# A hybrid decoder step on one core: token halves instead of quarters, another start of pair 1, and a written order for evictions, taps and weight parts

## Chip, cores and metric

One core of a Trainium2 chip runs the whole program. The metric is device time in microseconds (us), the median of several runs; a profile is one further execution. Engines: PE (matmul), PEld (its weight loads), DVE, ACT, POOL, and SP, whose queue issues all DMA transfers here.

## What is computed

One decoder layer for 1024 prompt tokens and 32 sample tokens (8 sequences of 4), 1056 columns in all, model width 1024. The part that the change touches is the end of the mixer and the feed-forward block:

```
x = x + (sig(gA)*A@w_br_ret + sig(gB)*B@w_br_sg + sig(gC)*C@w_br_x) @ w_o
z  = rmsnorm(x) @ w_up                    # 1024 -> 2*2816
zc = conv_b + sum(conv_w[j] * zp[:, j:j+L] for j in range(3))   # causal, zp = [history, z]
a, b = split(zc, 2)
x = x + (gelu(a) * b) @ w_down;  y = rmsnorm(x)
```

Outputs are y, the retention states, the last two rows of z for each sequence (the convolution's state), and the key/value caches.

## The kernel before

Activations lie transposed: 128 partitions of channels, tokens along the columns. Each fp32 product is made of three matmuls in the type fp32r: a value is cast to a high part (ACT), the rest is the low part (a subtraction, on POOL or DVE), and high*high, high*low, low*high are added up in PSUM. The helpers record most operations, so profile lines are theirs: mm is L106, act L109, vtt (DVE tensor-tensor) L112, ptt (POOL tensor-tensor) L115, stt (DVE scalar-tensor-tensor) L118, dma L103.

**Columns.** In the attention projection w_o (loop at L1337, two passes of eight output tiles) and in the up projection the 1056 columns are two halves of 528, each two quarters of 264 (256 prompt tokens and 8 sample tokens). So the residual tile x2c is read from DRAM and written to it (scx) by two DMAs a tile, one for the 256s and one for the 8s; the gated sum mg is split by two casts and two subtractions (split_q, L305); and an eviction of a product to z takes two operations, one for the prompt and one for the samples (z_put, L1400).

**Up projection.** Its 44 output tiles are taken as 22 pairs: tile j of a (gelu side) and tile 22+j of b. Pair 0 is a plain product. Pairs 1 to 21 use Winograd's form of Strassen's scheme: input rows in two halves, tokens in two halves, so seven products (prod, L1379) instead of eight. A product is 4 row blocks x 3 terms x 2 chunks = 24 matmuls. The weight blocks are a11, a12 (first slab), a21, a22 (second slab) and the sums s1 = a21+a22, s2 = s1-a11, s3 = a11-a21, s4 = a12-s2; the column operands are the plain blocks B11, B21, B12, B22 and T1 to T4 (differences of them, made once by t1, t2, t2l, t3 from L1480 and split by T1s, T3s, T4s). The products are, in this order, a11*B11, s2*T2, a12*B21, s3*T3, s1*T1, s4*B22, a22*T4. f_prep (L1298) loads nothing itself: it makes s1, s2 on DVE and s3, s4 on POOL, casts three pieces of 1024 columns and a22 on ACT, subtracts on POOL, and lets f_dma fetch the next pair's two slabs into the two buffers wr.

**PSUM and evictions.** A product has one of three PSUM buffers in turn (L1382), so a product waits for the eviction of the third one before it. a11 is evicted by ACT into p1 (first half of tile zt); s2 by DVE as r = s2 + p1 (second half of zt); s3 as u3 and s1 as u4 (tile zu), s1 once more into z of b, s4 into z of a, a22 into z of b, a12 into z of a.

**Convolution.** For each of the two tiles, ACT makes c = w2*z + bias (for 1024 prompt columns and 32 sample columns, L109) and copies the state columns; DVE adds two taps, each one operation of 1024 columns and one of 32 (L118); ACT applies gelu to the a side; DVE multiplies (c<-c, 1056 columns) and a DMA stores the result to sca.

**What sets the order.** In before, code order on each engine follows a small scheduler. convs and preps are queues of generators; after (L1591), called behind each product, advances convs by one or two steps, then preps by one, then up to four entries of todo. conv_a runs to the end (with gelu) before conv_b begins. For pair 0, todo (L1501) is a list of steps, one taken per row block of six matmuls; the steps that are left are run before pair 1, and T3s, T1s, T4s are put behind. In the last pair first_down (L1570) starts the down projection's loads.

Of the kernel before, what the change touches and what calls it, by code (L numbers as in the profile page):

```python
# [71 lines left out]
QW = 264  # L72
HW = 2 * QW

# [4 lines left out]
def step_kernel(ctx: ExitStack, tc: tile.TileContext, xT, memT, wslab, cst, ident_d, rope, vec, sgc, sgm, sgs,  # L79
# [215 lines left out]

    def q_parts(t):

        v = quarters(t)
        return v[:, :, 0:256], v[:, :, 256:QW]

    def t_parts(t):

        return t[:, 0:TP].rearrange("p (q c) -> p q c", c=256), t[:, TP:T].rearrange("p (q c) -> p q c", c=8)

    def split_q(src, name):  # L305

        hi = slot(name + "h", F32R)
        lo = slot(name + "l", F32R)
        for h, l, s in zip(q_parts(hi), q_parts(lo), t_parts(src)):
            nc.scalar.copy(out=h, in_=s)  # L310
            ptt(l, s, f(h), ALU.subtract)
        return hi, lo
# [57 lines left out]
    with tc.manual_schedule():  # L370
# [927 lines left out]
        def f_prep(j):  # L1298
            if j >= NFF:
                return  # L1300
            wa, wb = fraw.pop(j)
            a11, a12, a21, a22 = wa[:, 0:512], wa[:, 512:1024], wb[:, 0:512], wb[:, 512:1024]
            sa, sb = slot("fs"), slot("fs")
            s2, s3, s1, s4 = sa[:, 0:512], sa[:, 512:1024], sb[:, 0:512], sb[:, 512:1024]
            d = fw[j] = {}

            def parts(names, src):
                hi = wp.tile([P, 1024], F32R, tag="wh", name="wh", bufs=3)
                lo = wp.tile([P, 1024], F32R, tag="wl", name="wl", bufs=3)
                nc.scalar.copy(out=hi, in_=src)  # L1310
                ptt(lo, src, f(hi), ALU.subtract)
                for i, n in enumerate(names):
                    d[n] = (hi[:, 512 * i:512 * i + 512], lo[:, 512 * i:512 * i + 512])

            def sum12():
                vtt(s1, a21, a22, ALU.add)
                vtt(s2, s1, a11, ALU.subtract)

            def sum34():
                ptt(s3, a11, a21, ALU.subtract)  # L1320
                ptt(s4, a12, s2, ALU.subtract)

            def last22():
                t = slot("f22", F32R)
                nc.scalar.copy(out=t[:, 0:512], in_=a22)
                ptt(t[:, 512:1024], a22, f(t)[:, 0:512], ALU.subtract)
                d["a22"] = (t[:, 0:512], t[:, 512:1024])
                f_dma(j + 1)

            p0 = lambda: parts(("a11", "a12"), wa)  # L1330
            p1 = lambda: parts(("s2", "s3"), sa[:, 0:1024])
            p2 = lambda: parts(("s1", "s4"), sb[:, 0:1024])
            for fn in (p0, sum12, sum34, last22, p1, p2) if j == 1 else (sum12, sum34, p0, last22, p1, p2):
                fn()
                yield

        for half in range(2):  # L1337
            rate[0] = 0.25
            for m in range(8):
# [27 lines left out]
                for i, o in zip(q_parts(x2c[m]), t_parts(scx[m])):  # L1367
                    dma(o[:, 2 * half:2 * half + 2], i[:, 2 * half:2 * half + 2])
# [10 lines left out]
        def prod(w, name, ps=None, start=True, stop=True, tick=None):  # L1379

            if ps is None:
                ps = bpp.tile([P, 2, 512], F32, tag="bp", name="bp", bufs=3)  # L1382
            wh, wl = [x.rearrange("p (k c) -> p k c", c=P) for x in w]
            for k in range(4):
                xh, xl = xop(name, k)
                for i, (a, r) in enumerate(((wh, xh), (wh, xl), (wl, xh))):
                    for q in range(2):
                        mm(ps[:, q, 0:QW], a[:, k, :], r[:, q * QW:(q + 1) * QW], start=(start and k == 0 and i == 0),
# [10 lines left out]

        def z_put(ps, half, z, zs, tmp=None):  # L1400

            oz = z[:, 2 + 512 * half:514 + 512 * half].rearrange("p (q c) -> p q c", c=256)
            os_ = zs[:, 4 * half:4 * half + 4, 2:6].rearrange("p (q i) t -> p q i t", q=2)
            iz = ps[:, :, 0:256]
            is_ = ps[:, :, 256:QW].rearrange("p q (i t) -> p q i t", i=2)
            if tmp is None:
                nc.scalar.copy(out=oz, in_=iz)
                nc.scalar.copy(out=os_, in_=is_)
            else:
                tv = quarters(tmp)  # L1410
# [119 lines left out]
        while todo:  # L1530
            do()
# [391 lines left out]
```

## Time and profile before

| what | value |
|---|---|
| median of 3 runs | 1989.2 us (1988.41 to 1991.27) |
| profiled execution | 1988.9 us |
| its span, first to last instruction | 1987.1 us |
| mean granted TensorE clock | 0.988 |
| busy: PE / DVE / ACT / POOL | 95% / 53% / 31% / 47% of the span |
| HBM read, written | 137.04 MB, 35.43 MB |

The profile names operations by line and by tile: bp is the PSUM buffer of the up projection, mp that of the others; xh, xl are high and low parts of the column operands, wh, wl those of weights, f the split a22, wr raw weight slabs, fs the weight sums, z and zs up-projection results of prompt and samples, c the convolution's results, opr a result read back from sca, x (x2) the residual. In a timeline a row gives start, duration, engine, line, operation, out<-in, shapes, how many were merged, and in brackets how long the engine had been idle and what ended that.

### The profile page before, as it was taken

What the parts mean: (1) busy time and instruction counts of PE and PEld (TensorE: products, weight loads), DVE (VectorE), ACT (ScalarE), POOL (GpSimd) and SP (SyncE); (2) the same over time, 40 slices, a digit from 0 to 9 for tenths busy, and PEclk for the clock granted to TensorE, in tenths of its full rate; (3) what the DMA queues carried; (4) which work ended last, traced back from release to release, by engine and by line L of the source; (5) the groups of instructions that cost most, each with busy time, mean ns of one, the idle gap of its engine ahead of it and who ended that gap; (6) DMA issues with size and microseconds to landing.
All of it is one profiled execution on the core that took longest, in us unless ns stands there. A gap on an engine that the chain in (4) does not pass through costs nothing. (4 is left out here: it accounts for less than half of the span.)

```text
span 1987.1 us, 31577 instructions
## 1 busy us (share of the span) xinstructions
PE 1888.2 (95%) x13201; PEld 1854.9 (93%) x13201; DVE 1057.2 (53%) x1507; ACT 615.4 (31%) x962; POOL 927.9 (47%) x596
## 2 busy tenths in 40 slices
PE   7999999999899999999999998799999999899997
PEld 6999999999899999999999997699999999899996
DVE  8463636442555532111112268788888888744437
ACT  5223222422134432111222244344333434321104
POOL 7242433231633334333254465765666566664404
PEclk9999999999999999999999999899999999999999
DMA  5112131314132323111221641122222223642202
GB/s 180 54 43 88 43 110 43 120 55 149 59 133 99 97 87 97 43 43 43 99 84 43 205 128 54 65 65 65 65 80 82 65 70 100 230 140 99 95 1 88
DMA packets 65438, 174.52 MB, mean 88 GB/s; under 512 B 14288, under 2 KB 25712, under 8 KB 65296
## 3 DMA queue, kind: packets, MB, share of 16 engines
q1 hardware_dynamic: 65296, 172.50, 26.7%
q8 instruction: 104, 1.70, 0.4%
q14 instruction: 38, 0.31, 0.1%
HBM read 137.04 MB, written 35.43 MB: 87 GB/s over the span
## 5 line engine op out<-in xcount | busy, mean ns | idle before, releaser
L115 POOL TENSOR_TENSOR wl<-wr,wh 128x1024 fp32r<-128x1024 f32 x115 | 281.9, 2454 | 399.1 <-ACT wh L150 377.2
L106 PE MATMUL mp<-hh,wh 128*128 128x384 f32 (+1 forms) x1152 | 263.7, 337 | 9.9 <-ACT hh L109 5.0
L106 PE MATMUL mp<-hl,wh 128*128 128x384 f32 (+1 forms) x1152 | 254.0, 328 | 4.3 <-DVE hl L118 4.3
L106 PE MATMUL mp<-hh,wl 128*128 128x384 f32 (+1 forms) x1152 | 251.4, 326 | 0.0
L106 PE MATMUL bp<-xh,wh 128*128 128x264 f32 x1072 | 221.2, 288 | 24.2 <-DVE zt L112 16.1
L106 PE MATMUL bp<-xh,wl 128*128 128x264 f32 x1072 | 219.7, 286 | 6.7 <-POOL wl L115 6.7
L106 PE MATMUL bp<-xl,wh 128*128 128x264 f32 x1072 | 220.4, 287 | 5.1 <-DVE xl L112 3.5
L106 PEld LDWEIGHTS mp<-hh,wh 128*128 128x128 f32 x1152 | 192.4, 191 | 12.7 <-ACT rsh L351 5.1
L106 PEld LDWEIGHTS mp<-hl,wh 128*128 128x128 f32 x1152 | 193.5, 190 | 6.7 <-DVE hl L118 6.7
L106 PEld LDWEIGHTS bp<-xh,wh 128*128 128x128 f32 x1072 | 167.8, 190 | 28.9 <-DVE zt L112 19.9
L106 PEld LDWEIGHTS mp<-hh,wl 128*128 128x128 f32 x1152 | 193.5, 190 | 0.0
L118 DVE SCALAR_TENSOR_TENSOR c<-z,hist,c 128x1024 f32<-128x1024 f32 x88 | 154.9, 1760 | 50.0 <-ACT c L109 47.7
L106 PEld LDWEIGHTS bp<-xh,wl 128*128 128x128 f32 x1072 | 167.9, 190 | 7.4 <-POOL wl L115 7.4
L106 PEld LDWEIGHTS bp<-xl,wh 128*128 128x128 f32 x1072 | 167.5, 190 | 7.3 <-DVE xl L112 5.2
L112 DVE TENSOR_TENSOR x<-x,mp 128x288 f32<-128x288 f32 (+3 forms) x167 | 105.7, 675 | 122.2 <-PE mp L106 118.1
L115 POOL TENSOR_TENSOR wl<-fs,wh 128x1024 fp32r<-128x1024 f32 x42 | 113.3, 2698 | 50.3 <-ACT wh L1310 47.0
L150 ACT CAST wh<-wr 128x1024 fp32r<-128x1024 f32 x100 | 103.9, 1041 | 79.8 <-PE mp L106 50.0
L106 PE MATMUL mp<-ach,whs 128*128 128x384 f32 (+3 forms) x524 | 123.5, 325 | 4.8 <-DVE x L112 3.8
L106 PE MATMUL mp<-ach,wls 128*128 128x384 f32 (+3 forms) x524 | 123.5, 325 | 0.0
L106 PE MATMUL mp<-acl,whs 128*128 128x384 f32 (+3 forms) x524 | 123.0, 324 | 0.0
L112 DVE TENSOR_TENSOR th<-mp,rst 128x768 f32<-128x768 f32 (+1 forms) x48 | 31.7, 701 | 170.9 <-PE mp L106 150.3
L118 DVE SCALAR_TENSOR_TENSOR th<-th,mp 128x768 f32<-128x768 f32 (+1 forms) x48 | 31.7, 701 | 145.4 <-PE mp L106 145.4
(341 smaller groups left out, 4069.6 us busy)
## 6 DMA issues: line engine op xcount, KB each, us to landing
wr<-in_wslab SPq DMA_DIRECT2D x164, 512.0 KB, 3.6
sca<-c SPq DMA_DIRECT2D x22, 528.0 KB, 5.6
opr<-sca SPq DMA_DIRECT2D x22, 528.0 KB, 4.6
opr<-scr SPq DMA_DIRECT2D x16, 528.0 KB, 5.4
scr<-ort SPq DMA_DIRECT2D x8, 528.0 KB, 8.3
x<-scx SPq DMA_DIRECT2D x8, 528.0 KB, 10.6
s<-in_sret SPq DMA_DIRECT2D x8, 512.0 KB, 6.2
out_srets<-s SPq DMA_DIRECT2D x8, 512.0 KB, 3.5
```

The costliest lines, as they stand in the source:

```text
L106: nc.tensor.matmul(out=out, lhsT=l, rhs=r, start=start, stop=stop)
L112: nc.vector.tensor_tensor(out=out, in0=a, in1=b, op=op)
L115: nc.gpsimd.tensor_tensor(out=out, in0=a, in1=b, op=op)
L118: nc.vector.scalar_tensor_tensor(out=out, in0=a, scalar=s, in1=b, op0=op0, op1=op1)
L150: nc.scalar.copy(out=hi, in_=raw)
```

## The change

- Half 0 of the columns is now tokens 0 to 527, half 1 tokens 528 to 1023 and the 32 samples. x2c is loaded by one DMA a tile and stored by one a half; mg is split by one cast and one subtraction.
- Half 0 of z is one eviction of 528 columns. In half 1 the products on B12, B22 and T1 have chunks of 248 and 280 columns, so that prompt (2 x 248) and samples (32) are two operations; s1's eviction to u4 also becomes two.
- Pair 1 has its own code and product order: a11, a12, s4, s2, s3, s1, a22. todo goes on through its products. The sums of pair 1 are made on POOL, every second low part of half 1 as well, and all splits of T1, T3, T4; s1, s4 of pair 1 get buffers of their own (fh, fl). Since s4 comes first there, u4 is added to z of a by two extra additions later.
- Pairs 2 to 21 have a written order: tap steps of both tiles alternate with the evictions, the first step of conv b does not wait for gelu of conv a, and the four weight parts of the next pair stand behind a12, s1, s4 and at the head of the next pair. The next pair's slabs are fetched from there.
- In pair 21 the steps of first_down stand behind a12, s3, s1, s4 and a22 (before: behind a11, s2, a12, s3, s1).

DVE, a pair in the middle: the rows from the last eviction of one pair (z of a22) to the eviction of s2 (zt) in the next, before:

```order
L112 TENSOR_TENSOR z<-bp,zu 128x512
L112 TENSOR_TENSOR zs<-bp,zu 128x4x4
L118 SCALAR_TENSOR_TENSOR c<-z,hist,c 128x1024
L118 SCALAR_TENSOR_TENSOR c<-zs,hist,c 128x32
L118 SCALAR_TENSOR_TENSOR c<-z,hist,c 128x1024
L118 SCALAR_TENSOR_TENSOR c<-zs,hist,c 128x32
L118 SCALAR_TENSOR_TENSOR c<-z,hist,c 128x1024
L118 SCALAR_TENSOR_TENSOR c<-zs,hist,c 128x32
L112 TENSOR_TENSOR fs<-wr 128x512
L112 TENSOR_TENSOR fs<-fs,wr 128x512
L112 TENSOR_TENSOR zt<-bp,zt 128x528
```

And the same place now, up to the eviction of a12 (z<-bp,zt):

```order
L112 TENSOR_TENSOR z<-bp,zu 128x528
L118 SCALAR_TENSOR_TENSOR c<-z,hist,c 128x1024
L118 SCALAR_TENSOR_TENSOR c<-zs,hist,c 128x32
L118 SCALAR_TENSOR_TENSOR c<-z,hist,c 128x1024
L118 SCALAR_TENSOR_TENSOR c<-zs,hist,c 128x32
L112 TENSOR_TENSOR zt<-bp,zt 128x528
L118 SCALAR_TENSOR_TENSOR c<-z,hist,c 128x1024
L118 SCALAR_TENSOR_TENSOR c<-zs,hist,c 128x32
L112 TENSOR_TENSOR z<-bp,zt 128x528
```

zt moves ahead of conv b's first tap and of the weight sums, which now stand behind both of conv b's taps.

POOL at the start, from the first weight part of pair 1 (wl<-wr) on; xl are low parts of column operands, wl, fl and f of weights. Before:

```order
L115 TENSOR_TENSOR wl<-wr,wh 128x1024
L115 TENSOR_TENSOR fs<-wr 128x512
L115 TENSOR_TENSOR fs<-wr,fs 128x512
L115 TENSOR_TENSOR f_10993<-wr,f_10993 128x512
L115 TENSOR_TENSOR xl<-x2c,xh 128x528 x2
L115 TENSOR_TENSOR wl<-fs,wh 128x1024
L115 TENSOR_TENSOR xl<-x2c,xh 128x528 x4
L115 TENSOR_TENSOR wl<-fs,wh 128x1024
L115 TENSOR_TENSOR xl<-x2c,xh 128x528
L1417 MEMSET z 128x2
L1418 COPY zs<-hist 128x8x2
L115 TENSOR_TENSOR xl<-x2c,xh 128x528 x4
```

And now:

```order
L115 TENSOR_TENSOR wl<-wr,wh 128x1024
L115 TENSOR_TENSOR xl<-x2c,xh 128x528 x4
L115 TENSOR_TENSOR fl<-fs,fh 128x1024
L115 TENSOR_TENSOR wl<-fs,wh 128x1024
L115 TENSOR_TENSOR f_11148<-wr,f_11148 128x512
L115 TENSOR_TENSOR xl<-x2c,xh 128x528 x8
L1411 MEMSET z 128x2
L1412 COPY zs<-hist 128x8x2
L115 TENSOR_TENSOR xl<-x2c,xh 128x528 x4
L115 TENSOR_TENSOR wl<-wr,wh 128x1024
```

All weight parts of pair 1 stand ahead of the twelve xl of T3, T1 and T4, and the first part of pair 2 behind them; the sums moved ahead of this piece.

SP in pair 21: from the store of pair 19's result (sca) to the first loads of the residual (x), before:

```order
L103 DMA sca_10912<-c 128x1056
L103 DMA opr<-sca_10893 128x1056
L103 DMA opr<-sca_10894 128x1056
L103 DMA wr<-in_wslab 128x1024 x4
L103 DMA opr<-sca_10895 128x1056
L103 DMA opr<-sca_10896 128x1056
L103 DMA x_16286<-scx_192 128x1056
```

And now:

```order
L103 DMA sca_10872<-c 128x1056
L103 DMA opr<-sca_10853 128x1056
L103 DMA opr<-sca_10854 128x1056
L103 DMA wr<-in_wslab 128x1024 x4
L103 DMA sca_10873<-c 128x1056
L103 DMA opr<-sca_10855 128x1056
L103 DMA opr<-sca_10856 128x1056
L103 DMA x_16291<-scx_192 128x1056
```

The store of pair 20's result stands ahead of the residual now.

The diff, cut to its core:

```diff
-QW = 264
-HW = 2 * QW
+HW, QW = 528, 264
+HA, HB = 248, 280
...
-            mops.append(split_q(acc[m], "mg"))
+            mops.append(split(acc[m], "mg"))
...
-            for o, i in zip(q_parts(x2c[m]), t_parts(xT[m])):
-                dma(o, i)
+            dma(x2c[m], xT[m])
...
+            ch = ((0, 0, HA), (1, HA, HB)) if name in ("B12", "B22", "T1") else ((0, 0, QW), (1, QW, QW))
...
+        def put_t(ps, out, tmp):
+            vtt(n496(out), ps[:, :, 0:HA], n496(tmp), ALU.add)
+            vtt(out[:, 2 * HA:HW], ps[:, 1, HA:HB], tmp[:, 2 * HA:HW], ALU.add)
...
+            if half == 0:
+                put(ps, z[:, 2:2 + HW], tmp)
+                return
...
-        T1s = lambda k: x_split("T1", k, h(k, 0), vtt if k < 2 else ptt)
+        T1s = lambda k: x_split("T1", k, h(k, 0), ptt)
...
-            lambda: (norm_sums(1), one()), one, one, None, None, lambda: norm_root(1), one,
+            lambda: (norm_sums(1), f_sums(1, ptt)()), lambda: f_prep0(1), None, None, None, None, lambda: norm_root(1),
...
+        put(prod(d["a11"], "B11", tick=do), p1)
+        n = prod(d["a12"], "B21", tick=do)
...
+        n = prod(d["s4"], "B22", tick=do)
...
+        put(prod(d["s2"], "T2", tick=do), r, p1)
+        pa.first()
+        pa.tap(1)
+        put(prod(d["s3"], "T3", tick=do), u3, r)
...
-        for j in range(1, NFF):
+        for j in range(2, NFF):
...
+            f_prep3(j)
...
+            pb.first()
+            pa.tap(1)
...
+            put(prod(d["a11"], "B11"), p1)
+            ticks()
+            pa.tap(0)
+            pa.gelu()
+            put(prod(d["s2"], "T2"), r, p1)
+            ticks()
+            pb.tap(1)
             n = prod(d["a12"], "B21")
...
+                f_prep0(j + 1)
+            pb.tap(0)
+            s34 = None if last else f_sums(j + 1, vtt)
+            put(prod(d["s3"], "T3"), u3, r)
...
+                s34()
+            conv_end(j - 1, pa, pb)
             n = prod(d["s1"], "T1")
...
+                f_prep1(j + 1)
             n = prod(d["s4"], "B22")
             z_put(n, 1, *za, u4)
...
+            conv[0].first()
...
+                f_prep2(j + 1)
             n = prod(d["a22"], "T4")
             z_put(n, 0, *zb, u3)
```

Here first is the ACT step of a convolution, tap(1) and tap(0) its two DVE steps, conv_end the product and the store; f_prep0 to f_prep3 split (a11, a12), (s2, s3), (s1, s4) and a22, f_prep3 fetching the next slabs; f_sums makes s1, s2 and returns the function that makes s3, s4 on POOL.

More of the change, by code (lines that the diff above doesn't have):

```diff
@@ L1296, in f_dma, with f_parts @@
                     dma(t, wslab[SLABS.index(key)])
[L1298 to L1307, printed above, removed]
+        def f_parts(j, names, src, own=False):
+            if own:
+                hi, lo = slot("fh", F32R, [P, 1024]), slot("fl", F32R, [P, 1024])
+            else:
@@ L1319, in sum34 @@
[L1319 to L1335, printed above, removed]
+            nc.scalar.copy(out=hi, in_=src)
+            ptt(lo, src, f(hi), ALU.subtract)
+            for i, n in enumerate(names):
+                fw[j][n] = (hi[:, 512 * i:512 * i + 512], lo[:, 512 * i:512 * i + 512])
+        def f_quads(j):
+            return [t[:, 512 * i:512 * i + 512] for t in fraw[j] for i in range(2)]
@@ new lines, in step_kernel, with f_sums, f_prep0 @@
+        fsum = {}
+        def f_sums(j, sub):
+            a11, a12, a21, a22 = f_quads(j)
+            fsum[j] = (slot("fs"), slot("fs"))
+            s2, s3, s1, s4 = [t[:, 512 * i:512 * i + 512] for t in fsum[j] for i in range(2)]
+            sub(s1, a21, a22, ALU.add)
+            sub(s2, s1, a11, ALU.subtract)
+            return lambda: (ptt(s3, a11, a21, ALU.subtract), ptt(s4, a12, s2, ALU.subtract))
+        def f_prep0(j):
+            fw[j] = {}
+            f_parts(j, ("a11", "a12"), fraw[j][0])
@@ new lines, in f_prep1, with f_prep2, f_prep3 @@
+        def f_prep1(j, own=False):
+            f_parts(j, ("s2", "s3"), fsum[j][0][:, 0:1024], own)
+        def f_prep2(j, own=False):
+            f_parts(j, ("s1", "s4"), fsum[j][1][:, 0:1024], own)
+        def f_prep3(j):
+            a22 = f_quads(j)[3]
+            t = slot("f22", F32R)
+            nc.scalar.copy(out=t[:, 0:512], in_=a22)
+            ptt(t[:, 512:1024], a22, f(t)[:, 0:512], ALU.subtract)
+            fw[j]["a22"] = (t[:, 0:512], t[:, 512:1024])
+            del fraw[j]
+            f_dma(j + 1)
@@ L1366, in step_kernel @@
                     vtt(s, s, sq[:, 0:HW], ALU.add)
[L1367 to L1368 removed]
+                dma(scx[m][:, half * HW:(half + 1) * HW], hs(m, half))
             drain()
@@ L1464, in ticks @@
                 wait.pop(0)[1]()
-        def turn_to(q, n):
-            for _ in range(n):
-                turn(q)
         h = hs
@@ new lines, in step_kernel, with first_down @@
+        pb.tap(0)
+        conv_end(0, pa, pb)
+        def first_down():
+            a_load(0)
+            a_load(1)
+            w_dma()
+            w_dma()
+            yield
+            a_split(0)
+            w_prep()
+            yield
+            a_split(1)
+            w_prep()
+            yield
+            a_load(2)
+            a_load(3)
+            x2_load(range(4))
+            yield
+            x2_load(range(4, 8))
+            yield
+        for j in range(2, NFF):
+            last = j == NFF - 1
+            pa, pb = conv
+            if j == 2:
+                pa.first()
+            d = fw[j]
+            f_prep3(j)
+            fw.pop(j)
+            pb.first()
+            pa.tap(1)
+            p1, r, u3, u4 = blocks(j)
```

255 lines of the change are left out of this document (111 added, 144 removed).

## The prediction

> **What bounds the kernel now.** I read the page first, for the busy share of each engine, then the waits of PE, a table by stretches, and the timelines of one pair, of the start and of the end. An execution took 1988.9 us with the profiler on: this span and 1.8 us around it.
>
> ```profile
> span 1987.1 us, 31577 instructions
> ...
> PE 1888.2 (95%) x13201; PEld 1854.9 (93%) x13201; DVE 1057.2 (53%) x1507; ACT 615.4 (31%) x962; POOL 927.9 (47%) x596
> ```
>
> PE is busy 95% of the span, so only its idle time and its slow time can be won. The waits of PE in the whole run (us in total, times, longest) say what ends that idle time:
>
> ```profile
> PE bp L106 <- DVE zt L112: 16.1, 18, 0.9
> ...
> PE bp L106 <- POOL wl L115: 6.7, 3, 3.9
> ...
> PE bp L106 <- ACT wh L1310: 5.3, 1, 5.3
> ...
> PE bp L106 <- DVE zu L112: 4.1, 2, 3.8
> ...
> PE mp L106 <- POOL mgl L115: 1.2, 1, 1.2
> ```
>
> The first comes 18 times at 0.9 us: once a pair. The next three are a few long waits. The table by stretches places them: from the end of the attention projection to pair 3, pairs 3 to 20, pair 21, and the first down-projection group.
>
> ```profile
> 1197.90:1294.00 96.10, 74.75 (x531) 71.29 (x532) 80.35 (x87) 40.74 (x73) 61.27 (x37) 0.91 0.16 52
> 1294.00:1685.50 391.50, 375.42 (x3028) 370.20 (x3028) 324.74 (x396) 152.67 (x249) 245.53 (x180) 1.00 0.24 73
> 1685.50:1709.50 24.00, 21.16 (x171) 20.58 (x170) 20.16 (x23) 10.47 (x19) 14.67 (x9) 1.00 0.35 113
> 1709.50:1726.00 16.50, 12.68 (x76) 12.17 (x77) 12.49 (x13) 6.57 (x9) 10.19 (x4) 1.00 1.03 399
> ```
>
> The first stretch has PE idle for 21 of 96 us, at a granted clock of 0.91: the long waits stand there, and DVE is busy 80 us of it. In the second PE is idle only by the short wait. The PE timeline gives the marks: pair 3 begins at 1294.20, pair 21 at 1685.47, the down projection at 1709.41.
>
> ```profile
> 1294.20 0.40 PE L106 MATMUL bp<-xh,wh 128*128 128x264 f32 x2
> ...
> 1425.20 0.40 PE L106 MATMUL bp<-xh,wh 128*128 128x264 f32 x2
> ...
> 1435.89 0.40 PE L106 MATMUL bp<-xh,wl 128*128 128x264 f32 x2
> 1437.20 0.51 PE L106 MATMUL bp<-xh,wh 128*128 128x264 f32 x2 [0.90 <-DVE zt L112]
> ...
> 1685.47 0.41 PE L106 MATMUL bp<-xh,wh 128*128 128x264 f32 x2
> ...
> 1709.41 0.72 PE L106 MATMUL mp<-ach,whs 128*128 128x384 f32 x3 [0.96 <-DVE zs L112]
> ```
>
> A pair takes (1685.47 - 1294.20)/18 = 21.74 us. From 1425.20 to 1435.89 lie 44 rows of two matmuls, 0.1215 us each, so a product (24) takes 2.92 and seven 20.4. The row at 1437.20 starts 1.31 after the one before instead of 0.24, and its first two matmuls take 0.1 longer: the wait costs 1.17 a pair, and a pair without it takes 20.57. It is s1 waiting for a PSUM buffer: three are in turn, and s1 needs the one from which DVE evicts s2 into zt.
>
> **Why that eviction is late, and what DVE and POOL share.** Rows of the same pair on ACT, DVE and POOL, in order of time:
>
> ```profile
> 1423.37 1.24 ACT L109 ACTIVATE c<-z,hist 128x1024 f32<-128x1024 f32 x1 [7.44 <-DVE zs L112]
> ...
> 1425.36 1.28 DVE L118 SCALAR_TENSOR_TENSOR c<-z,hist,c 128x1024 f32<-128x1024 f32 x1
> ...
> 1426.14 2.76 POOL L115 TENSOR_TENSOR wl<-fs,wh 128x1024 fp32r<-128x1024 f32 x1 [1.70 <-ACT wh L1310]
> ...
> 1426.55 2.40 DVE L118 SCALAR_TENSOR_TENSOR c<-zs,hist,c 128x32 f32<-128x32 f32 x1
> ...
> 1428.86 1.29 POOL L115 TENSOR_TENSOR fs<-wr 128x512 f32<-128x512 f32 x1
> 1428.87 2.36 DVE L118 SCALAR_TENSOR_TENSOR c<-z,hist,c 128x1024 f32<-128x1024 f32 x1
> ...
> 1433.75 1.28 DVE L118 SCALAR_TENSOR_TENSOR c<-z,hist,c 128x1024 f32<-128x1024 f32 x1 [2.36 <-ACT c L109]
> ...
> 1434.95 0.25 DVE L118 SCALAR_TENSOR_TENSOR c<-zs,hist,c 128x32 f32<-128x32 f32 x1
> ...
> 1435.11 0.69 DVE L112 TENSOR_TENSOR fs<-wr 128x512 f32<-128x512 f32 x1
> ...
> 1436.44 0.70 DVE L112 TENSOR_TENSOR zt<-bp,zt 128x528 f32<-128x528 f32 x1
> ...
> 1438.98 2.42 POOL L115 TENSOR_TENSOR wl<-wr,wh 128x1024 fp32r<-128x1024 f32 x1
> ...
> 1439.74 2.78 DVE L112 TENSOR_TENSOR c<-c 128x1056 f32<-128x1056 f32 x1
> ...
> 1441.36 2.31 POOL L115 TENSOR_TENSOR f<-wr,f 128x512 fp32r<-128x512 f32 x1
> ```
>
> PE finished s2 about 1430.3; the eviction (zt, 1436.44) stands in DVE's queue behind three taps, of which one waited 2.36 us for ACT, and the weight sums. Read next how DVE and POOL exclude each other. The tap of 32 columns (1426.55) takes 2.40 and ends at 1428.95, as POOL's wl ends at 1428.90; the next tap (1428.87) ends 1.08 after POOL's fs, where alone it takes 1.28; the product c (1439.74) ends 1.12 after wl; POOL's f ends 1.15 after c, and the wl of 1426.14 ends 2.26 after the tap of 1425.36. So a DVE operation with both inputs in SBUF and a POOL subtraction run one after the other, in turns, and wait whole. Evictions (zt, zu, z: one input in PSUM) are not held up. The Trainium skill, page "SBUF — State Buffer", section "Who interferes with whom", says the same: the two share a port as an exclusive lock, held for a whole instruction, and a DVE operation with one SBUF input does not contend. That speaks against a change that only reorders this work.
>
> **The steady pair.** Nothing is taken from DVE or POOL here but one small eviction a pair. The work under the exclusion, at the durations above: POOL 3 x 2.42 + 2 x 1.29 + 1.2 and 0.3 of small copies = 11.3; DVE 4 x (1.28 + 0.16, the start of 1435.11 less that of 1434.95) + 1.25 + 2 x 0.69 = 8.4; together 19.7 of the 20.57 that PE needs. DVE has 5.6 of evictions besides. So the order decides, and I lay it out, from the eviction of s4 (time 0) on. ACT's first convolution step lets tap 1 of conv a begin at 1.4 (1.24 by the row of 1423.37, and the hand-overs); a22's eviction lies in that wait. Tap and its 32 columns 2.85, tap 0 4.1, POOL's wl 6.4, the 32 columns and POOL's f 7.6 with zt inside it at 7.1, tap 1 of conv b with a POOL copy 9.0, eviction of a12 9.7, tap 0 10.95, wl 13.2, POOL's fs 14.45, two sums 15.85, eviction of s3 16.55 with POOL's second fs under it until 17.1, the product c 18.2, four evictions of s1 19.8, s4 20.6. The loop of DVE and POOL is 20.6 long, as long as PE's. PE's own dates are kept: s2 is done at about 6 and evicted by 7.1 instead of 6 us late, s3 may stay until a22 begins at 17.5, s1 until 20.5. Weights: fs of the next pair need the second slab, whose load starts when POOL's f ends (7.6) and has until 14.4. If POOL's first wl gets in before tap 0, zt and all behind it is 0.6 later: 21.2. Bounds: 20.57 (PE), and 21.4 (two such turns lost beside the 20.6, less what slack is left). I take 20.75: 18 x (21.74 - 20.75) = 17.8 us less.
>
> Pair 21 takes 1709.41 - 1685.47 = 23.94. 3.37 of it is above 20.57; about 1 of that is the first matmul of the down projection, which waits for the last eviction in both orders, and stays. The wait for zt (1.2) goes, and 0.6 of the others: 1.8 less (0.5 to 2.2).
>
> **The narrow chunks.** Three of seven products now run 248 and 280 columns for 264 and 264. No row has a 248. The nearest narrow ones, of 128 columns with a smaller weight block, between two other matmuls each:
>
> ```profile
> 589.62 0.22 PE L106 MATMUL ap<-vch,p 128*64 128x128 f32 x1
> ...
> 590.34 0.22 PE L106 MATMUL ap<-vch,p 128*64 128x128 f32 x1
> ```
>
> They are the first and the last of 13 in turn, twelve starts apart in 0.72: 0.06 us each, half of the 0.1215 of 264 columns. Time goes with columns, and the sum of columns is the same: 0. If no matmul went below the 0.118 that 256 columns would take, it were 36 x 0.004 = 0.15 a pair; it is in the bounds.
>
> **The start.** The same exclusion, at its worst:
>
> ```profile
> 1227.93 7.39 POOL L115 TENSOR_TENSOR wl<-fs,wh 128x1024 fp32r<-128x1024 f32 x1 [6.53 <-ACT wh L1310]
> ...
> 1235.28 7.12 POOL L115 TENSOR_TENSOR xl<-x2c,xh 128x528 fp32r<-128x528 f32 x4
> ```
> ```profile
> 1199.91 0.71 DVE L112 TENSOR_TENSOR ns<-ssq,ns 128x528 fp32r<-128x528 f32 x1 [0.70 <-ACT ns L1262]
> ...
> 1230.55 2.55 DVE L112 TENSOR_TENSOR x2c<-x2c 128x528 f32<-128x528 f32 x4
> ...
> 1233.03 3.37 DVE L118 SCALAR_TENSOR_TENSOR c<-z,hist,c 128x1024 f32<-128x1024 f32 x1
> ```
>
> POOL's wl (s2, s3), alone 2.4 us, takes 7.39 since DVE runs one operation after another until the tap of 1233.03; PE waits 3.9 for it, with only a11 between. Now a11, a12 and s4 (8.8 us, on operands of pair 0 and on a weight part split earlier) stand ahead of s2, the taps of pair 0 move behind the T operands, and all twelve T subtractions go to POOL, in a row: 12 x 1.28 = 15.4 us. So s3, s1 and a22 will wait for POOL instead. The work under exclusion until pair 3 bounds it: DVE 37 operations of 528 columns at 0.63 (four in 2.55 at 1230.55), 8 taps with their 32 columns at 1.3, two products c at 1.15, four sums at 0.65 = 38.6; POOL seven wl at 2.3, sixteen xl at 1.25, 5.5 fs at 1.25, two f at 1.2 = 45.4; with 2.2 of evictions behind the last c: 86.2 us from 1199.9, thus 1286 if nothing ever idles, and 1288 with 2 us of waits. Against 1294.2 that is 6 less. The bounds: 12 less (1282: taps that slip behind the start of pair 3) and 2 more (the 3.8 us of work that went from DVE to POOL, unhidden).
>
> **The end and the rest.** The loads of the residual move behind s4 and a22 (before: s3 and s1), and the store of pair 20's result now stands ahead of them. The SP queue and PE's wait:
>
> ```profile
> 1684.94 22.25 SPq L103 DMA_DIRECT2D wr<-in_wslab  x4
> ...
> 1708.23 5.31 SPq L103 DMA_DIRECT2D x<-scx  x8
> ```
> ```profile
> 1725.36 0.72 PE L106 MATMUL mp<-ach,whs 128*128 128x384 f32 x3 [3.23 <-DVE x L112]
> ```
>
> The residual is not held by its place but by the four wr loads before it, the last of which went out at about 1707 and had waited for POOL. That is 21.7 into a pair of 23.94. Now POOL's f ends at 7.6, ACT's casts let the first split begin at 8.6, and four splits of 2.42 with two DVE turns of 1.1 end at 20.5, in a pair of 22.1: 0.6 later against the pair's end, so 0.6 more (0 to 3). The store waits for c of pair 20, done long before. One subtraction in place of two for mg: of the 1.2 us that PE waits for mgl, 0.4 less. The merged loads and stores of x2c save SP issues under which no wait stands: 0.
>
> Sum: -6 - 17.8 - 1.8 + 0.6 - 0.4 = -25.4; 1988.9 - 25.4 = 1963.5. The median of the three runs is 0.3 above the profiled execution; I say 1963.
>
> **Rivals.** (1) PE becomes the bound everywhere: zt is the one eviction that was late, and the waits of DVE for ACT (2.36) go. Steady 20.57: 21.1 less; the start 12, pair 21 2.2, mg 0.4: 1953. Against it stands the 19.7 of 20.57. (2) The exclusion takes the gain: period 21.4 (6.1 less), no gain at the start, 0.5 in pair 21, 1.5 more at the end: 1984. For it: the POOL chain of T operands and the tie at tap 0. (3) Slower: in my layout POOL holds up DVE for 5.8 of its 11.3 us a pair. DVE's own 14.8 (8.4, 5.6 and 0.8 for ACT) and 6.9 of POOL make 21.74: from there on each pair is longer than now. With 7.7, as when one more wl and no eviction beside it falls in DVE's way, a pair takes 22.5: 18 x 0.76 = 13.7 more, 3 at the start, 1 at the end: 2006. By the Trainium skill's rule of the lock taken for all of POOL's work it would be worse still; the rows show turns and evictions beside it. (4) The order written changes nothing where it counts, because zt merely gives way to zu: 1988.
>
> **How the numbers follow.** Forecast 0.55 (1956 to 1974), (1) 0.18, (2) 0.15, (3) 0.08, (4) 0.04. The range 1951 to 1985 takes in the forecast, (1) to its floor and (2), and leaves out (3), (4) and a little. 0.2% (4 us) is about what a measurement can tell from no change: faster 0.88, the same 0.04, slower 0.08.
>
> **What would show it.** Right: no PE wait for zt in the pairs, a period of 20.6 to 20.9 between a11 starts, pair 3 at 1282 to 1292, a wait for xl (POOL) in place of the one for wl in pair 1, and, if PE waits in the pairs, for zu. DVE's tap rows would be longer than now. Wrong: a period over 21.3 with DVE waits on POOL, or pair 3 after 1294; matmuls of 248 columns further apart than 0.118; a wait for x in the down projection over 5 us.

## The result and the profile after

The changed kernel takes 1966.55 us, the median of four runs (1963.83 to 1969.01); before, 1989.2. The ratio is 0.9884, 95% interval 0.9867 to 0.9901: 1.2% faster, 22.6 us. The forecast was 1963, range 1951 to 1985. The profiled execution took 1969.0 us, the longest of the four, so the sums below (its span against that of before, 19.9 us) are at the small end of the gain.

The page's span and busy times, and the waits of PE in the whole run (us in total, times, longest):

```profile
span 1967.2 us, 31365 instructions
...
PE 1885.8 (96%) x13201; PEld 1856.8 (94%) x13201; DVE 1071.7 (54%) x1480; ACT 615.6 (31%) x954; POOL 963.2 (49%) x594
```
```profile
PE mp L106 <- DVE x L112: 8.3, 3, 4.2
...
PE bp L106 <- POOL xl L115: 5.9, 7, 2.8
PE bp L106 <- DVE zu L112: 5.5, 2, 3.5
...
PE bp L106 <- POOL wl L115: 2.1, 2, 1.8
...
PE bp L106 <- DVE zt L112: 0.4, 1, 0.4
```

The wait for zt, 18 times before, is down to one of 0.4, ahead of pair 3. POOL's xl has taken the place of its wl as a wait at the start. At the top now stands x, the residual of the down projection.

The table by stretches, with the same marks as before (start; pairs 3 to 20; pair 21; the first 16.5 us of the down projection). The columns are the stretch, its length, busy time (and count) of PE, weight loads, DVE, ACT, POOL, then PE's granted clock, the DMA engines' share and GB/s:

```profile
1198.99:1291.20 92.21, 76.60 (x532) 72.54 (x533) 71.05 (x79) 39.26 (x67) 63.88 (x42) 0.91 0.12 40
1291.20:1658.26 367.06, 367.06 (x3024) 367.06 (x3025) 347.58 (x380) 153.85 (x253) 274.88 (x181) 1.00 0.25 80
1658.26:1679.70 21.44, 20.55 (x171) 20.37 (x169) 19.83 (x20) 11.68 (x20) 17.78 (x11) 1.00 0.41 128
1679.70:1696.20 16.50, 12.30 (x58) 12.04 (x59) 5.89 (x9) 5.21 (x10) 2.73 (x2) 0.79 1.00 383
```

In the pairs PE is busy for all of the 367.06 us: 20.39 a pair for 21.74. The last row is the opposite: 58 matmuls in the time in which 76 ran before, at a clock of 0.79 instead of 1.00. Stretch by stretch, by the marks in PE's timeline:

| stretch | before | after | forecast | measured |
|---|---|---|---|---|
| up to the first matmul of pair 0 | 1197.9 | 1199.0 | -0.4 | +1.1 |
| pair 0 to pair 3 | 96.3 | 92.2 | -6 | -4.1 |
| pairs 3 to 20 | 391.3 | 367.1 | -17.8 | -24.2 |
| pair 21 | 23.9 | 21.4 | -1.8 | -2.5 |
| down projection to the end | 277.7 | 287.5 | +0.6 | +9.8 |

The first row moves between executions of the same code: from 1197.7 to 1200.0 in the kernels below that are changed from after, and alike up to there. Pair 0 to pair 3 takes 90.9 to 93.3 in the five kernels with after's code up to pair 3 (after among them), so its 4.1 carries about 1 us; pairs 3 to 20 take 367.0 to 367.8 in the six with after's code for them. Two rows are far from the forecast, in opposite directions.

A pair in the middle of after (its first a11 starts at 1495.16), DVE's timeline from the last eviction of the pair before, and POOL's first weight part in it:

```profile
1494.74 0.18 DVE L112 TENSOR_TENSOR zs<-bp,zu 128x32 f32<-128x32 f32 x1
...
1498.83 2.40 DVE L118 SCALAR_TENSOR_TENSOR c<-zs,hist,c 128x32 f32<-128x32 f32 x1
1501.21 0.71 DVE L112 TENSOR_TENSOR zt<-bp,zt 128x528 f32<-128x528 f32 x1
...
1504.08 0.71 DVE L112 TENSOR_TENSOR z<-bp,zt 128x528 f32<-128x528 f32 x1 [0.41 <-PE bp L106]
...
1510.68 0.70 DVE L112 TENSOR_TENSOR zu<-bp,zt 128x528 f32<-128x528 f32 x1
1511.30 1.95 DVE L112 TENSOR_TENSOR c<-c 128x1056 f32<-128x1056 f32 x1
```
```profile
1497.68 3.49 POOL L115 TENSOR_TENSOR wl<-fs,wh 128x1024 fp32r<-128x1024 f32 x1 [2.37 <-ACT wh L1285]
```

Counted from the end of s4's eviction (1494.92), zt is done at 7.0 (laid out in the prediction: 7.1), a12 at 9.9 (9.7), s3 at 16.5 (16.55), the product c at 18.3 (18.2). zt starts 6.05 after the first a11; before it started 11.2 after (1436.44 - 1425.20). POOL's wl has the place between the taps that the layout gave it: the tap of 32 columns (1498.83) ends with it.

DVE's taps of 1024 columns over pairs 3 to 20, before and then after (busy us and mean ns, then the idle time ahead of them):

```profile
L118 DVE SCALAR_TENSOR_TENSOR c<-z,hist,c 128x1024 f32<-128x1024 f32 x72 | 123.9, 1721 | 42.3 <-ACT c L109 42.3
```
```profile
L118 DVE SCALAR_TENSOR_TENSOR c<-z,hist,c 128x1024 f32<-128x1024 f32 x72 | 101.8, 1414 | 4.6 <-ACT c L109 4.6
```

DVE's wait for ACT, 2.36 a pair, is nearly gone. The taps as a whole are longer, as the prediction said, 10.9 us a pair for 9.9: those of 1024 columns became shorter, those of 32 columns longer (93.8 us in all for 55.1).

### The profile page after: what moved, and what is told of

The parts are those of the page before. It is cut to its first block, busy times and chain, and to the rows that moved or that the text cites. A ratio compares the mean times of both kernels' runs of the same rounds, so it can differ in the third digit from the quotient of the medians.

```text
span 1967.2 us, 31365 instructions
## 1 busy us (share of the span) xinstructions
PE 1885.8 (96%) x13201; PEld 1856.8 (94%) x13201; DVE 1071.7 (54%) x1480; ACT 615.6 (31%) x954; POOL 963.2 (49%) x594
## 4 chain that ended last, share of the span: by engine, by line
PE 77%; DVE 9%; issue 5%; ACT 3%; POOL 3%; DMA 2%; SPq 0%; DVEq 0%; POOLq 0%; ACTq 0%
PE mp L106 53%; PE bp L106 19%; PE ap L106 4%; DVE c L118 1%; POOL wl L115 1%; POOL mgl L115 1%; DVE hl L118 1%; DVE s L112 1%; ACT sw L476 1%; DMA xr<-in_xT 1%; DVE x2c L118 1%; DMA scr<-ox 0%; POOL xl L115 0%; DVE rt L118 0%; DVE st L526 0%
## 5 line engine op out<-in xcount | busy, mean ns | idle before, releaser
L115 POOL TENSOR_TENSOR wl<-wr,wh 128x1024 fp32r<-128x1024 f32 x115 | 296.5, 2581 | 425.5 <-ACT wh L150 378.4
L106 PE MATMUL bp<-xl,wh 128*128 128x264 f32 (+2 forms) x1056 | 217.3, 288 | 6.1 <-POOL xl L115 5.7
L106 PE MATMUL bp<-xh,wh 128*128 128x264 f32 (+2 forms) x1056 | 216.5, 286 | 6.1 <-DVE zu L112 3.5
L106 PE MATMUL bp<-xh,wl 128*128 128x264 f32 (+2 forms) x1056 | 216.3, 286 | 2.1 <-POOL wl L115 2.1
L115 POOL TENSOR_TENSOR wl<-fs,wh 128x1024 fp32r<-128x1024 f32 x41 | 123.8, 3020 | 51.4 <-ACT wh L1285 51.3
L118 DVE SCALAR_TENSOR_TENSOR c<-z,hist,c 128x1024 f32<-128x1024 f32 x88 | 134.2, 1526 | 17.8 <-ACT c L109 17.8
```

The source lines that it names most:

```text
L106: nc.tensor.matmul(out=out, lhsT=l, rhs=r, start=start, stop=stop)
L115: nc.gpsimd.tensor_tensor(out=out, in0=a, in1=b, op=op)
L118: nc.vector.scalar_tensor_tensor(out=out, in0=a, scalar=s, in1=b, op0=op0, op1=op1)
```

## Experiments

Three kernels ask what made the pairs faster, two how much room is left in them, five where the start and the end lost. Each ratio is against the kernel before on the same chip; its medians there were 1990.5 to 1991.6, 0.1% above the 1989.2 of the result, so differences in us between kernels measured beside different runs of before carry 1 to 2 us. Times within a pair come from the profile; pair times are the difference of two a11 starts.

**zt back in its old place.** In after, for pairs 2 to 21:

```diff
-            put(prod(d["s2"], "T2"), r, p1)
+            n = prod(d["s2"], "T2")
             ticks()
             pb.tap(1)
+            s34 = None if last else f_sums(j + 1, vtt)
+            put(n, r, p1)
             n = prod(d["a12"], "B21")
...
             pb.tap(0)
-            s34 = None if last else f_sums(j + 1, vtt)
```

> The changed kernel with one thing put back: in pairs 2 to 21 the eviction of s2 (zt) and the two weight sums before it stand behind conv b's first tap again, as before the change. Theory (the place of zt is the lever): zt starts about 12 us after the pair's first a11 matmul, s1 waits about 1 us for the PSUM buffer, the period of pairs 3 to 20 goes from 20.38 to 21.4-21.9, the whole to 1985-1991. Rival (the fewer evictions of token halves, or the spread of weight parts on POOL, made the gain): period 20.4-20.8, whole 1967-1974.

Measured: 2011.6 us, ratio 1.0097 (1.0080 to 1.0114): slower than before. PE's wait for zt in the whole run, a wait of DVE ahead of zt, and the first matmuls of pairs 4 and 21:

```profile
PE bp L106 <- DVE zt L112: 37.3, 15, 3.3
```
```profile
1511.07 0.69 DVE L112 TENSOR_TENSOR fs<-wr 128x512 f32<-128x512 f32 x1 [0.74 <-DMA wr<-in_wslab]
```
```profile
1316.49 0.40 PE L106 MATMUL bp<-xh,wh 128*128 128x264 f32 x2
...
1706.48 0.40 PE L106 MATMUL bp<-xh,wh 128*128 128x264 f32 x2
```

(1706.48 - 1316.49)/17 = 22.94 a pair, in a pattern of pairs of about 22.3, 25.5 and 20.4. That is slower than both the theory and the rival. The edit moves two things, zt and the two sums in front of it, and the sums now wait for the second slab of weights, 25.4 us in the 18 pairs from 3 to 20 (0.74 in the row above); in before and in after DVE waits for no slab there. So zt and the sums at their old place, with the rest of the change kept, are worse than before; how much of it is zt's place alone was not separated. The expected 21.4 to 21.9 left out the wait for the slab: without its 1.4 a pair, 22.94 would be about 21.5, an estimate that takes each such wait as lost in full.

**zt moved in before.** The mirror image, with nothing else of the change:

```diff
             put(n, p1)
-            after(2)
+            after(2 if j == 1 else 1, j == 1)
             n = prod(d["s2"], "T2")
             put(n, r, p1)
-            after()
+            after(1 if j == 1 else 2)
```

The second argument says whether a step of the weight parts runs there.

> The kernel before with one thing moved: behind a11 only one step of the convolutions and no step of the weight parts, behind s2 two steps of the convolutions, so that DVE evicts s2 (zt) ahead of conv b's first tap and the sums. Everything else is as before (quarters, start, end). Theory (the place of zt is the lever): no PE wait for zt, period 20.4-20.8 instead of 21.74, whole 1967-1973. Rival 1 (halves and the spread weight parts are needed as well): 21.3 or more, whole 1982 or more. Rival 2 (the weight parts, now one step later, come too late): PE waits for wl or wh instead, period above 21.7, whole above 1989.

Measured: 1985.08, ratio 0.9975 (0.9963 to 0.9986). PE's first a11 of pairs 3 and 21, and what it waits for in between:

```profile
1295.05 0.40 PE L106 MATMUL bp<-xh,wh 128*128 128x264 f32 x2
...
1491.58 0.51 PE L106 MATMUL bp<-xh,wl 128*128 128x264 f32 x2 [0.93 <-POOL wl L115]
...
1523.95 0.48 PE L106 MATMUL bp<-xh,wh 128*128 128x264 f32 x2 [0.48 <-DVE zs L112]
...
1679.61 0.40 PE L106 MATMUL bp<-xh,wh 128*128 128x264 f32 x2
```

A pair takes (1679.61 - 1295.05)/18 = 21.36. The wait for zt is gone, and two others came: in every second pair s2 waits for its low part (wl), and in the others s4 for the eviction of a12 (zs), which now stands behind the sums. The waits are those of rival 2 (wl) and the size is that of rival 1 (21.3 or more, 1982 or more): the weight parts have to move as well. An early zt is worth 0.38 a pair as long as the weight parts come late.

**zt moved in before, and the weight parts spread.** The parts get the places of after, everything else stays: quarters, start, end.

```diff
-            for fn in (p0, sum12, sum34, last22, p1, p2) if j == 1 else (sum12, sum34, p0, last22, p1, p2):
+            first = lambda: (p0(), sum12())
+            if j == 1:
+                fns = (p0, sum12, sum34, last22, p1, p2)
+            elif j == 2:
+                fns = (sum12, sum34, p0, last22, p1, p2)
+            else:
+                fns = (first, sum34, p1, p2, last22)
+            for fn in fns:
...
-            after(2)
+            after(2 if j == 1 else 1, j == 1)
             n = prod(d["s2"], "T2")
             put(n, r, p1)
-            after()
+            after(1, j == 1)
```

> The kernel before with the eviction of s2 (zt) moved ahead of conv b's first tap, as in the first such run, and with the weight parts of the next pair at the places of the changed kernel: (a11, a12) and the sums s1, s2 behind a12, s3 and s4 behind s3, (s2, s3) behind s1, (s1, s4) behind s4, a22 behind a22. Quarters, start and end are those of before. Theory (the steady gain is the place of zt and the spread of the weight parts, nothing else): period 20.4-20.6 in pairs 3 to 20, no PE wait for wl there, whole 1966-1970. Rival (the fewer evictions of token halves are needed too): 20.9 or more, whole 1975 or more.

Measured: 1968.26, ratio 0.9883 (0.9869 to 0.9896), as much as the whole change. Pairs 3 and 21 start at:

```profile
1294.30 0.40 PE L106 MATMUL bp<-xh,wh 128*128 128x264 f32 x2
...
1518.59 0.52 PE L106 MATMUL bp<-xh,f 128*128 128x264 f32 x2 [0.99 <-DVE zu L112]
...
1665.66 0.48 PE L106 MATMUL bp<-xh,wh 128*128 128x264 f32 x2
```

17 pairs take 20.53 to 20.57; one takes 21.96 (the wait at 1518.59). Apart from that one pair the theory's numbers hold. So two moves make the steady gain: zt ahead of conv b's first tap, and weight parts spread over the pair; the spread alone, in before, was not run. What after has beyond that, halves of tokens and a written order, is worth 20.55 - 20.39 = 0.16 a pair and the one hiccup, 4 to 5 us over the run; which of the two gives it was not separated. Start and end here are those of before: the end, from the first matmul of the down projection on, takes 277.8.

**How much room a pair has left.** Two kernels add work to after that changes no value, in pairs 4 and up: the sum s1 three times on DVE, or the low part of (s2, s3) twice on POOL.

```diff
-            sub(s1, a21, a22, ALU.add)
+            for _ in range(3 if j > 3 else 1):
+                sub(s1, a21, a22, ALU.add)
```
```diff
-            ptt(lo, src, f(hi), ALU.subtract)
+            for _ in range(2 if j > 3 and names[0] == "s2" else 1):
+                ptt(lo, src, f(hi), ALU.subtract)
```

> The changed kernel with the sum s1 computed three times instead of once in pairs 4 and up, which adds two DVE operations of 128x512 with both inputs in SBUF, 1.3 us a pair, ahead of the eviction of s3. Theory as in the prediction (DVE and POOL fill 20.6 of a pair, no slack): period 21.2-21.8. Rival (PE is the bound by a margin of more than 1.3): 20.4-20.6.

> The changed kernel with the subtraction of the weight part (s2, s3) done twice on POOL in pairs 4 and up, which adds 2.4 us of POOL a pair. Theory (no slack in what DVE and POOL share): period 22 or more. Rival (what is left of slack is more than 2.4, since POOL fills gaps in which DVE evicts): 20.4-20.8.

Pairs 5 and 21 of the first (1979.2 us in its one run) and of the second (1985.4 in its one run):

```profile
1331.62 0.48 PE L106 MATMUL bp<-xh,wh 128*128 128x264 f32 x2
...
1671.33 0.48 PE L106 MATMUL bp<-xh,wh 128*128 128x264 f32 x2
```
```profile
1331.93 0.48 PE L106 MATMUL bp<-xh,wh 128*128 128x264 f32 x2
...
1673.62 0.48 PE L106 MATMUL bp<-xh,wh 128*128 128x264 f32 x2
```

(1671.33 - 1331.62)/16 = 21.23 and (1673.62 - 1331.93)/16 = 21.36: 1.3 us on DVE cost 0.84 of them, 2.4 on POOL cost 0.97. On DVE the period is at the low edge of the theory's 21.2 to 21.8, on POOL it lies between theory and rival: the pair is not without slack, as the theory had it, and it is far from having 1.3. About 0.45 is free for DVE. That is less than what DVE waits for PE in a pair of after (its groups in pairs 3 to 20, the 18 evictions of a22 and the 18 of a12):

```profile
L112 DVE TENSOR_TENSOR z<-bp,zu 128x528 f32<-128x528 f32 x18 | 12.7, 707 | 7.3 <-PE bp L106 7.3
L112 DVE TENSOR_TENSOR z<-bp,zt 128x528 f32<-128x528 f32 x18 | 12.7, 707 | 6.6 <-PE bp L106 6.6
```

(7.3 + 6.6)/18 = 0.77 of a pair. The half of it ahead of a22's eviction lies under ACT's first convolution step, for which the next tap waits anyway; the 0.37 ahead of a12's is close to the 0.45. DVE's loop is nearly full, and PE, not it, ends the pair by half a microsecond.

**The residual's loads earlier.** In after's first_down, which issues the loads of the down projection in pair 21:

```diff
             a_split(0)
             w_prep()
             yield
-            a_split(1)
-            w_prep()
-            yield
             a_load(2)
             a_load(3)
             x2_load(range(4))
+            a_split(1)
+            w_prep()
             yield
             x2_load(range(4, 8))
             yield
+            yield
```

> The changed kernel with the first four loads of the residual and the readback of results 2 and 3 put ahead of the second weight part of the down projection in pair 21, so that they no longer stand behind the last load of wr and the store of pair 20's result. Theory (their place in SP's queue made the down projection 8 to 9 us longer): the first PE wait for x falls from 4.2 to under 1, the matmuls behind it run at full clock, the whole falls by 4 to 8, to 1959-1963. Rival (the loads wait for their buffers or for the transfers, not for the queue): within 1.5 of 1966.6.

Measured: 1958.79, ratio 0.9839 (0.9825 to 0.9854), 7.8 us below after. SP's queue in after, then in this kernel (start, duration from the first to the last of the group):

```profile
1659.62 19.15 SPq L103 DMA_DIRECT2D wr<-in_wslab  x4
1678.83 0.42 SPq L103 DMA_DIRECT2D sca<-c  x1
1679.35 1.78 SPq L103 DMA_DIRECT2D opr<-sca  x2
1681.22 6.15 SPq L103 DMA_DIRECT2D x<-scx  x8
```
```profile
1658.33 13.19 SPq L103 DMA_DIRECT2D wr<-in_wslab  x3
...
1672.57 1.89 SPq L103 DMA_DIRECT2D x<-scx  x4
```

In after's down projection, which starts at 1679.70, DVE waits for the loads, and PE for DVE's addition of a product to the residual:

```profile
1688.45 1.32 DVE L112 TENSOR_TENSOR x<-x,mp 128x768 f32<-128x768 f32 x2 [8.90 <-DMA x<-scx]
```
```profile
1689.92 1.22 PE L106 MATMUL mp<-ach,whs 128*128 128x384 f32 x3 [4.20 <-DVE x L112]
1690.94 1.08 PE L106 MATMUL mp<-ach,wls 128*128 128x384 f32 x3
...
1696.14 0.65 PE L106 MATMUL mp<-ach,wls 128*128 128x384 f32 x3
...
1708.84 0.71 PE L106 MATMUL mp<-ach,whs 128*128 128x384 f32 x3 [2.59 <-DVE x L112]
...
1710.04 1.08 PE L106 MATMUL mp<-acl,whs 128*128 128x384 f32 x3
```

The first four loads go out 8.7 us earlier (the other four move up too, from behind a22 to behind s4), the wait of 4.20 is gone, and the end takes 1956.0 - 1678.40 = 277.6, as before the change. The theory holds: late loads are most of what the end lost.

Of the 9.8 in after's execution, 4.5 are waits for x (8.3 in three waits, for 3.8 in two before) and 2.8 are slow matmuls behind them. Behind the wait of 4.20 PE runs at little more than half speed for 6 us, until 1696.14: a group of three starts every 0.88 (1690.94 is the second of them) instead of 0.48, 2.8 us lost. Behind the wait of 2.59 it loses 1.6, and before lost as much behind one of 3.23. The other 2.5 come in the last 26 us, where PE runs slow once more; 1.5 of them stand in this kernel too, so they are not the loads'. The Trainium skill, page "TensorE: Matmul & The Clock Gate", section "What's actually happening", says that an idle window of about 3.4 us halves PE's clock and a busy one of 3.4 restores it. These rows agree that a wait is followed by a slow stretch that ends by itself, at 0.88/0.48 = 1.8 instead of 2. The window does not agree: the wait of 2.59 at 1708.84 is followed by a slow stretch too, and the same wait in this kernel is not (1699.48, where the next groups start 0.48 apart).

```profile
1699.48 0.72 PE L106 MATMUL mp<-ach,whs 128*128 128x384 f32 x3 [2.59 <-DVE x L112]
...
1700.53 0.65 PE L106 MATMUL mp<-acl,whs 128*128 128x384 f32 x3
```

What decides whether a short wait slows the clock stays open. The end varies with it: with after's order of loads it took 282.5 to 287.5 in the five executions profiled (after, zt back, the two with added work, the split shared below). The wait of 2.59 itself is not the loads': it stays here, where they are early, and its addition stands behind two taps of the last convolution in DVE's queue. Nor does every late load cost as much: with zt and the weight parts moved in before, the loads go out 0.8 us after the down projection begins (1.2 ahead of it in before), PE's first wait is 2.30, and the end still takes 277.8.

**The store behind the loads.** Which of the things in front of the loads held them? In after, the store of pair 20's result put behind them:

```diff
-            conv_end(j - 1, pa, pb)
+            if last:
+                vtt(pb.c, pb.c, pa.c, ALU.mult)
+                later(4, lambda o=sca[j - 1], c=pb.c: dma(o, c))
+            else:
+                conv_end(j - 1, pa, pb)
```

> The changed kernel with the store of pair 20's result put behind the eight loads of the residual instead of ahead of them. Theory (the loads are late because the last load of wr is late, and the readbacks; the store itself costs its issue, 0.5): the first PE wait for x in the down projection stays above 3, the whole falls by 1.5 at most. Rival (the store, waiting for the product c, held up the loads): the wait falls under 1.5, the whole by 4 or more.

Measured: 1962.53, ratio 0.9857 (0.9843 to 0.9870), 4.0 below after. The queue again, and PE's first wait for x (the down projection starts at 1679.86):

```profile
1678.98 0.90 SPq L103 DMA_DIRECT2D opr<-sca  x2
1679.97 5.15 SPq L103 DMA_DIRECT2D x<-scx  x8
```
```profile
1687.68 0.72 PE L106 MATMUL mp<-ach,whs 128*128 128x384 f32 x3 [1.80 <-DVE x L112]
```

Between the two theories, nearer the rival: the wait falls by 2.4. The store did not wait for c; it went out at once when the last wr had. But with it in front the loads start 1.4 later against the down projection: the two readbacks take 1.78 instead of 0.90, besides the store's own 0.42. That repeats: with the store in front the readbacks take 1.69 to 1.78 in five kernels, without it 0.86 to 0.90 in seven. The other 1.0 of the 2.4 comes behind the first load: the eight take 6.15 instead of 5.15, and the first lands 1.0 later. Whether that is the store's doing is not shown, since without a store ahead the eight took 5.15 to 6.79 in four kernels. The rest of the first wait's growth (0.59 before, 4.20 after) is 1.2. It fits the last load of wr, which went out 2.2 ahead of the down projection before and 0.9 ahead of it now.

**The T operands shared.** In after, every second low part of T1, T3 and T4 on DVE:

```diff
-        T1s = lambda k: x_split("T1", k, h(k, 0), ptt)
-        T3s = lambda k: x_split("T3", k, h(k, 1), ptt)
-        T4s = lambda k: x_split("T4", k, h(k + 4, 0), ptt)
+        T1s = lambda k: x_split("T1", k, h(k, 0), ptt if k % 2 else vtt)
+        T3s = lambda k: x_split("T3", k, h(k, 1), ptt if k % 2 else vtt)
+        T4s = lambda k: x_split("T4", k, h(k + 4, 0), ptt if k % 2 else vtt)
```

> The changed kernel with every second subtraction of the T1, T3 and T4 splits on DVE instead of POOL (6 of 12). Theory (DVE and POOL take turns, so what counts is the sum of both, and DVE needs 0.63 where POOL needs 1.28): start 3 to 4 us shorter (pair 3 at 1287-1288), whole 1962-1964. Rival 1 (POOL's chain alone is the bound and DVE stands idle): 6 to 8 shorter, whole 1958-1961. Rival 2 (the start is set by taps, ACT and evictions): within 1.5.

Measured: 1960.08, ratio 0.9846 (0.9832 to 0.9861), 6.5 below after. The start, pair 0 to pair 3, in its table by stretches:

```profile
1200.05:1287.66 87.61, 72.30 (x533) 69.36 (x533) 79.75 (x86) 39.80 (x68) 58.88 (x36) 0.94 0.13 45
```

87.6 instead of 92.2: 4.6 us. Six operations at 1.28 - 0.63 make 3.9, the theory's figure, and half of POOL's chain would have made 6 to 8. The 4.6 lies between, nearer the theory; as the start scatters by 1 us either way, that the sum over both engines is what counts is likely, and not shown. The whole came out below the theory's 1962 because of the end, which took 282.5 for 287.5. There PE's first wait is shorter, and no slow stretch follows it (it does follow one of 2.58, later):

```profile
1685.76 0.72 PE L106 MATMUL mp<-ach,whs 128*128 128x384 f32 x3 [3.48 <-DVE x L112]
```

That part is scatter. The next kernel has 87.4 for the start.

**Both.** The loads earlier and the T operands shared, with the two diffs above.

> The changed kernel with both improvements: the first four loads of the residual ahead of the second weight part of the down projection, and every second subtraction of T1, T3, T4 on DVE. Theory (they act at two places that do not share work): the gains add up, 1951-1955. Rival (the split on DVE gained at the end by chance, not at the start only): 1955-1958.

Measured: 1954.37, ratio 0.9814 (0.9801 to 0.9828): 12.2 below after, 1.9% below before, the fastest kernel here. The theory holds. The medians' gains, 7.8 and 6.5, would make 14.3; the 2.1 that is missing fits what the shared split had gained at the end by scatter. In the profile 4.8 lie at the start (1285.46 - 1198.09 = 87.4), 8.9 at the end (278.6).

**A next wait that only moved.** In the kernel with both, PE waits longest at the start for the eviction of a12, which stands behind the T operands in DVE's queue. A last kernel puts (T3's second half, T1) behind a12's product:

```diff
-            lambda: (t3(0), t3(1)), lambda: (T3s(0), T3s(1)), lambda: (T1s(0), T1s(1)), lambda: (t3(2), t3(3)), None,
-            lambda: (T3s(2), T3s(3)), None, lambda: (T1s(2), T1s(3)), None, None, None, lambda: T4s(0), None,
-            lambda: T4s(1), None, lambda: T4s(2), None, lambda: T4s(3)])
+            lambda: (t3(0), t3(1)), lambda: (t3(2), t3(3)), lambda: (T3s(0), T3s(1)), None, None, None, None, None,
+            lambda: (T3s(2), T3s(3)), None, lambda: (T1s(0), T1s(1)), lambda: (T1s(2), T1s(3)), lambda: T4s(0), None,
+            lambda: T4s(1), None, lambda: T4s(2), lambda: T4s(3)])
```

> The kernel with both improvements, and in pair 1 the splits of T3 (second half) and T1 put behind the product a12, so that DVE evicts a12 (z) before them. The profile of the kernel without this has PE waiting 5.6 us for that z, before s3. Theory (the wait is that eviction's place in DVE's queue): the wait falls under 2, pair 3 starts 3 to 5 earlier (1281-1283), whole 1949-1952. Rival (T3 and T1 then come too late by the same amount): the wait moves to xl or zu, whole 1953-1956.

Measured: 1955.24, ratio 0.9821 (0.9807 to 0.9834), no gain. The wait before and after this edit:

```profile
1246.46 0.81 PE L106 MATMUL bp<-xh,wh 128*128 128x264 f32 x2 [5.60 <-DVE z L112]
```
```profile
1255.40 0.51 PE L106 MATMUL bp<-xl,f 128*128 128x264 f32 x2 [3.66 <-DVE xl L112]
```

The rival was right: pair 1 is shorter (26.8 for 28.7), but its last product now waits for T4's low part, and pair 2 takes 30.6 for 27.8, at a clock of 0.90 for 0.95. Pair 3 starts no earlier.

## Why the prediction came out right, and where it did not

The time was 3.6 us above the forecast, within its range; the total was better than its terms, since two large errors cancelled. That is luck.

**The bound and the lever** were named rightly: one eviction behind DVE's taps, and the work of DVE and POOL in turns. Putting zt and the sums back loses all of the gain and more, part of it in a wait for weights; the layout of the pair held to 0.3 us at every date that can be compared. What the prediction did not see is that zt alone is not enough. It priced the change as one new order, while it is two moves, and once zt is moved the second (weight parts spread) carries most of it: 0.38 a pair without it, 1.19 with it.

**Steady pairs, -24.2 for -17.8.** The step that failed is "I take 20.75", and below it the floor of 20.57; 20.39 lies below both, and below the stated 20.6 to 20.9. That floor was the period less the one wait that the waits table names. The rest of before's products hold more such time: a22's second matmul starts 0.10 late as well, and s4 and a12 are 0.05 and 0.02 longer than in after. Seven products at the quoted step make 20.4, which is what after takes; this sum stood in the prediction and was not used as the floor. The loop of 20.6 was treated as full; it has 0.45 of slack. In the pair laid out above, DVE waits 0.41 for PE ahead of a12's eviction, where the layout had no such wait. Rival 1 (PE is the bound) describes the pairs, though not the run.

**Pair 21, -2.5 for -1.8.** 0.2 of the difference is the same floor. The rest is waits that the prediction left standing: of the 3.37 above the floor one wait is left, 0.9 ahead of the down projection's first matmul.

**Start, -4.1 for -6.** Right in kind: PE's long wait for wl became waits for xl (5.9 us in seven), zu and wl, and pair 3 starts at 1291.2, within the stated 1282 to 1292. The "2 us of waits" on top of the exclusive work were mis-sized: counted in the same way (1291.2, less the 1.05 by which this execution starts later, against 1286) they are 4. The part named as a cost, twelve subtractions in a row on POOL, is one: sharing them gives 4.6 back.

**The end, +9.8 for +0.6 (0 to 3).** This is the step that failed: "0.6 later against the pair's end, so 0.6 more". Against the pair's end the last load of wr is 1.3 later, since the pair is shorter than the 22.1 laid out. The date itself was good: POOL's four splits end 20.2 into pair 21, laid out 20.5. But two things behind it were set at nothing. The store, whose c was "done long before", delays the loads by 1.4 although it waits for nothing. And waits that are 4.5 longer in sum cost 7.3, because PE's clock falls behind them. The last 2.5 of the 9.8 are not explained by the loads. As a sign of being wrong the prediction had named a wait for x of over 5 us; 4.2 was below it and still the largest error.

**mg and the narrow chunks.** The wait for mgl is 1.0 for 1.2, where 0.4 less was forecast; no gain shows above the scatter of the first row. The chunks of 248 and 280 columns cost nothing: rows of two matmuls, one of each width, start 0.24 apart, as with 264.

```profile
1486.42 0.40 PE L106 MATMUL bp<-xh,wh 128*128 128x248 f32 x2
1486.66 0.41 PE L106 MATMUL bp<-xl,wh 128*128 128x248 f32 x2
```

**Rivals.** The period of (2), 21.4, is about that of the first of the two moves alone (21.36), and the 22.5 of (3) is near that of the rest without it (22.94). The sizes agree, the causes do not: in the first PE waited for wl and for an eviction behind the sums, in the second DVE waited for a slab ahead of zt. That either rival's mechanism is at work is not shown.

## What to carry over

When one late eviction is the wait, ask what the order behind it feeds: here the weight parts had to move with it. zt alone gave less than a third of the steady gain, and the spread weight parts with zt and the sums late were worse than before. Take the floor of a stage from its products times their step, not from its period less the waits that a table names. And when a stage gets faster, recompute the date of every load for the next one against the new end, with all that is issued ahead of it; here 4.5 us more of waiting cost 7.3, the difference being PE's clock behind the waits.

## What was not expected of the hardware

A DVE order that exchanges turns with POOL hides part of what is added: 2.4 us more on POOL cost a pair 0.97, 1.3 more on DVE 0.84. A store that waits for nothing, ahead of two loads in SP's queue, went with 1.69 to 1.78 for these two in five kernels, against 0.86 to 0.90 without it in seven. And PE ran at little more than half speed for 4 to 6 us after waits of 4.2 and, in some kernels, of 2.6, but not after one of 3.48.
